# A hybrid decoder block on one core: low parts of the convolution weights by accumulating transfers, heads' products out of their banks by ScalarE

## The chip, the core and the metric

The kernel runs on one core of a Trainium2 chip. A core has five engines with a queue of instructions each: TensorE (PE) multiplies matrices into PSUM banks, VectorE (DVE), ScalarE (ACT) and GpSimd (POOL) work element by element, and SyncE (SP) mostly issues transfers. Transfers can be issued from several queues; here nearly all go out from SP, and a few from POOL. Each queue is worked off in order, and an instruction that waits for a semaphore holds up all behind it on the same engine. The metric is the time of one execution on the device in microseconds (us); the median of the runs counts.

## The reference

The block takes x of 512 positions by 1024 channels, float32, and computes

```
h   = RMSNorm(x);  P = h @ W_in
yA  = B * causal_dwconv3(C * x_in)                      short gated convolution, 512 channels
yB  = NSA(q, compressed / selected / window keys)       8 heads of 64, 2 key groups
x   = x + W_o( sigmoid(gA) * (yA @ W_A) + sigmoid(gB) * (yB @ W_B) )
x   = x + W_down( silu(causal_dwconv3(W_g RMSNorm(x)) + b) * (W_u RMSNorm(x)) )
```

W_in yields B, C, x_in, the queries, keys and values, the branch gates and the two merge gates gA and gB. Each of the convolution's twelve weight tiles (four channel tiles i, three factors j) is 1024 input rows by 128 columns, 512 KB.

## The kernel before, in words

**Two parts of each number.** All dense products are taken with float32 values that are split in two: a high part in a reduced format (fp32r), and a low part, the difference. A product is three matmuls: weight high by input high (L403), weight high by input low (L404), and, after all of these for the tile, weight low by input high (L406). So a tile of 1024 rows needs its high part for the first 16 matmuls of 512 columns and its low part only for the last eight.

**Weight tiles up to the merge.** `load_w` (L124 to 133) loads a raw tile from SP into one of three raw buffers (`wr`, L126), copies it on ACT to the high part (`wh`, two buffers in turn, L130), and subtracts raw minus high for the low part (`wl`, two buffers, L128 and L132). The subtraction runs on DVE, or on POOL with `pool=True`. For the convolution (`conv_tile`, L690) the first two tiles in order of their number, a00 and a01, use DVE and the other ten POOL; the gates (`gate_tile`, L713) and the first merge product (`mix_a_pair`, L722) use POOL always. A low buffer can be written again only when PE has ended the eight L406 matmuls of the tile two before.

**Another way, in use further on.** `dma_split` (L153 to 157) serves the last stage, the feed-forward part: ACT writes the high part (L155) and the negated raw tile into the low part's buffer (L156, with scale -1, which rounds to the reduced format); then POOL issues a transfer (L157) that reads the weights again from memory and adds them to what stands in the buffer.

**Stages.** From 0 to about 62 us three rounds of the token projection (`tok_round`, L235) fill four banks each; round 0 and round 1 hold the heads' products, 128 by 384 a bank, which leave their banks for the array `a_all` at L341 to 346 (round 0) and in `evac` (L513 to 519, round 1): banks 0 and 2 by ACT, 1 and 3 by DVE. `heads` (L534) then normalises and rotates queries and keys on DVE, takes a power -1/2 on POOL (L366), transposes on PE (L565, tiles `pqt`) and splits them into high and low parts (L570 to 576, `kL` the keys' low part). `compress` (to L504) makes the compressed keys (`kc` at L496 and L497 are its parts). From 70 to 155 us the convolution's tiles run, in the order j = 1, 2, 0 for each i, so a01, a02, a00, a11, a12, a10 and so on. The attention (`attend`, L586) is issued ahead of them in the program and its operations are laid among the matmuls of the convolution and of the gates until 312 us. Then come the second merge product (`pmb`, weights `wh_bo`, loaded by `ring_w`, L166 to 171, in buffers of a pool that opens when the attention's pool closes), the output product, and from 390 us on the feed-forward part.

**What sets the order.** The kernel is built under a context that schedules by a simulated timeline: the order of the instructions on each engine follows from that simulation and not from the text alone. Any change of an operation's engine or kind can therefore move operations of other stages on all engines.

Of the kernel before, what the change touches and what calls it, by code (L numbers as in the profile page):

```python
# [11 lines left out]
F32 = mybir.dt.float32  # L12
F32R = mybir.dt.float32r
I32 = mybir.dt.int32
AF = mybir.ActivationFunctionType
# [4 lines left out]
D = 1024  # L20
# [41 lines left out]
N_AB = 384  # L62
# [20 lines left out]
def tile_block(ctx: ExitStack, tc: tile.TileContext, xT, pos, par, par2, w_tok, w_a3, w_gate, w_ao, w_bo, w_o,  # L83
               w_ff, w_dn, c_w1, out):
    nc = tc.nc
# [25 lines left out]
    def d_bank(name):  # L111
        return bank("d", name, 2)
# [8 lines left out]
        return bank("o", name, 1)  # L121


    def load_w(src, n, name, pool=False):  # L124

        raw = pa.tile([P, TOKC], F32, name=f"wr_{name}", tag="wr", bufs=NWR)  # L126
        hi = hi_tile(name)
        lo = pa.tile([P, D], F32R, name=f"wl_{name}", tag="wl", bufs=2)  # L128
        nc.sync.dma_start(raw[:, 0:n], src)
        nc.scalar.activation(hi[:, 0:n], raw[:, 0:n], AF.Copy)  # L130
        e = nc.gpsimd if pool else nc.vector
        e.tensor_sub(lo[:, 0:n], raw[:, 0:n], hi[:, 0:n].bitcast(F32))  # L132
        return hi, lo

    def load_taps(src, name):
# [17 lines left out]
    def dma_split(h, l, raw, src, dst=None):  # L153

        nc.scalar.activation(h, raw, AF.Copy)  # L155
        nc.scalar.activation(l, raw, AF.Copy, scale=-1.0)  # L156
        nc.gpsimd.dma_start(l if dst is None else dst, src, accum_op=ALU.add)  # L157
# [32 lines left out]
    def hi_tile(name):  # L190
        n_hi.append(name)
        i = 1 - len(n_hi) % 2
        return pa.tile([P, TOKC], F32R, name=f"wh_{name}", tag=f"wh{i}", bufs=1)
# [143 lines left out]
    banks_a = tok_round(0, first_slot)  # L337
# [2 lines left out]
    nc.vector.tensor_add(sq_sum[0][:, 0], sq_sum[0][:, 0], sq_sum[0][:, 1])  # L340
    for t in range(NT):  # L341
        dst = a_all[:, t * 12 * HD + N_AB:(t + 1) * 12 * HD]
        if t % 2 == 0:
            nc.scalar.activation(dst, banks_a[t][:, 0:N_AB], AF.Copy)
        else:
            nc.vector.tensor_copy(dst, banks_a[t][:, 0:N_AB])

    ident = const([P, P], "ident")
    make_identity(nc, ident)
# [50 lines left out]
    def dense(acc, units, first=True, last=True):  # L400

        for i, (wh, wl, xh, xl) in enumerate(units):
            nc.tensor.matmul(acc, wh, xh, start=first and i == 0, stop=False)  # L403
            nc.tensor.matmul(acc, wh, xl, start=False, stop=False)  # L404
        for i, (wh, wl, xh, xl) in enumerate(units):
            nc.tensor.matmul(acc, wl, xh, start=False, stop=last and i == len(units) - 1)  # L406

    def w_units(w, xh, xl, nk, k0=0, koff=0):
        wh, wl = w
        return [(wh[:, (koff + k) * P:(koff + k + 1) * P], wl[:, (koff + k) * P:(koff + k + 1) * P],  # L410
                 xh[:, k0 + k, :], xl[:, k0 + k, :]) for k in range(nk)]
# [101 lines left out]
    def evac(banks):  # L513
        for t in range(NT):
            dst = a_all[:, t * 12 * HD:t * 12 * HD + N_AB]
            if t % 2 == 0:
                nc.scalar.activation(dst, banks[t][:, 0:N_AB], AF.Copy)
            else:
                nc.vector.tensor_copy(dst, banks[t][:, 0:N_AB])

    def values(tt, acc):
        r = r1[:, tt:tt + 1]
# [164 lines left out]
    def f_tile(name):  # L687
        return pm.tile([P, S + 2], F32, name=name, tag="f", bufs=NF_T)

    def conv_tile(i):  # L690
        accs = []
        for j in (1, 2, 0):
            w = load_w(w_a3[2 + 3 * i + j], D, f"a{i}{j}", pool=3 * i + j > 1)
            acc = d_bank(f"pa{i}{j}")
            dense(acc, w_units(w, xg_h, xg_l, KD))
            if j == 1:
                cs_ = f_tile(f"cs{i}")[:, 0:S]
                nc.vector.tensor_mul(cs_, acc, r1sq)
            elif j == 2:
                u = f_tile(f"u{i}")  # L700
                nc.gpsimd.memset(u[:, 0:2], 0.0)
                nc.vector.tensor_mul(u[:, 2:], acc, cs_)
                t = f_tile(f"ct{i}")[:, 0:S]
                causal_conv(t, u, par_sb[:, CAW + 3 * i:CAW + 3 * i + 3])
                nc.gpsimd.tensor_mul(t, t, r1b)
            else:
                nc.vector.tensor_mul(t, acc, t)
                nc.scalar.activation(ya_h[:, i, :], t, AF.Copy)
                nc.vector.tensor_sub(ya_l[:, i, :], t, ya_h[:, i, :].bitcast(F32))
# [1 line left out]


    def gate_tile(j, t):  # L713
        w = load_w(w_gate[j], D, f"g{j}", pool=True)
        acc = d_bank(f"pg{j}")
        dense(acc, w_units(w, xg_h, xg_l, KD))
        nc.vector.tensor_mul(t, acc, r1b)
        nc.scalar.activation(t, t, AF.Tanh, scale=0.5)
# [3 lines left out]
    def mix_a_pair(i):  # L722
        for j in (2 * i, 2 * i + 1):
            mix_a[j] = f_tile(f"ma{j}")[:, 0:S]
            gate_tile(j, mix_a[j])
        w = load_w(w_ao[i], D, f"ao{i}", pool=True)
        for n, j in enumerate((2 * i, 2 * i + 1)):
            acc = d_bank(f"pma{j}")
            dense(acc, w_units(w, ya_h, ya_l, 4, koff=4 * n))
            nc.vector.scalar_tensor_tensor(mix_a[j], mix_a[j], 1.0, acc, op0=ALU.add, op1=ALU.mult)  # L730
# [43 lines left out]
    for i in range(4):  # L774
# [3 lines left out]
        w = ring_w(w_bo[i], f"bo{i}")  # L778
# [33 lines left out]
    for n, j in enumerate(O_ORDER):  # L812
        w = ring_w(w_o[j], f"o{j}")
# [261 lines left out]
```

## Time and profile before

| | |
|---|---|
| time, median of three runs | 727.26 us (726.14 to 728.48) |
| the profiled execution's own time, and its span | 729.73 us, 728.0 us |
| mean granted TensorE clock | 0.994 |
| PE busy | 715.6 us (98%) |
| DVE, ACT, POOL busy | 542.7 (75%), 426.4 (59%), 196.2 us (27%) |
| POOL, low parts of the convolution (L132) | ten of 2350 to 2688 ns, 24.5 us |
| DMA, mean rate over the span | 138 GB/s |

The profile comes from one execution of its own; the span runs from its first to its last instruction. "L132" is a line of the kernel above. In a row of the waits stand the engine that waits, its tile and line, who ended the wait, the sum in us, how often, and the longest. A row of the timeline has start, length, engine, line, operation, the tiles (written <- read), and in brackets the idle time ahead with its releaser. PEld is the load of weights into TensorE, which overlaps the matmuls. A matmul's length in the timeline is its latency; the next one starts before it ends.

### The profile page before, as it was taken

How to read it: one execution, taken by the hardware profiler on the slowest of the kernel's cores; microseconds unless marked ns; L12 is line 12 of the kernel's file. 1: busy time of each engine (PE TensorE's matmuls, PEld its weight loads, DVE VectorE, ACT ScalarE, POOL GpSimd, SP SyncE). 2: the span in 40 equal slices, each digit the busy share in tenths (PEclk: the TensorE clock that was granted, in tenths of full speed). 3: DMA queues.
4: the chain of work that ended last, by engine and by line, in shares of the span. 5: the costliest groups of instructions: out<-in, count | busy, mean ns of one | idle time of the engine just before them, and what ended most of it. 6: DMA issues, size and time to landing. Idle time of an engine off the chain costs nothing.

```text
span 728.0 us, 11411 instructions
## 1 busy us (share of the span) xinstructions
PE 715.6 (98%) x4309; PEld 638.0 (88%) x4309; DVE 542.7 (75%) x977; ACT 426.4 (59%) x724; POOL 196.2 (27%) x176
## 2 busy tenths in 40 slices
PE   9999998999999999989999999999999999999997
PEld 9999877888888888868789999999999999999986
DVE  6987998776566676446696879998787877878643
ACT  8525532886577687433575777666655566656530
POOL 3232544333433344316111212211221112211110
PEclk9999999999999999989999999999999999999999
DMA  7323322111122111052666699897878768795575
GB/s 269 97 91 124 109 87 86 59 59 58 59 75 70 59 59 59 1 202 87 206 168 147 147 226 206 230 205 188 196 185 215 194 166 211 172 219 108 114 144 149
DMA packets 39703, 100.24 MB, mean 138 GB/s; under 512 B 3808, under 2 KB 9056, under 8 KB 39648
## 3 DMA queue, kind: packets, MB, share of 16 engines
q1 hardware_dynamic: 26528, 70.41, 29.1%
q0 software_dynamic: 12832, 28.84, 23.1%
q8 instruction: 34, 0.56, 0.3%
q10 hardware_dynamic: 288, 0.26, 0.1%
q14 instruction: 21, 0.17, 0.1%
HBM read 97.40 MB, written 2.10 MB: 137 GB/s over the span
## 4 chain that ended last, share of the span: by engine, by line
PE 87%; DVE 6%; ACT 2%; DMA 2%; issue 2%; POOL 2%; ACTq 0%; DVEq 0%; POOLq 0%; SPq 0%
PE p L403 8%; PE p L404 8%; PE p L406 8%; PE pdn L406 5%; PE pdn L404 5%; PE pdn L403 5%; PE pg L403 4%; PE pg L404 4%; PE pg L406 4%; PE pt L653 2%; PE pa L406 2%; PE pa L404 2%; PE po L406 2%; PE pa L403 2%; PE po L403 2%
## 5 line engine op out<-in xcount | busy, mean ns | idle before, releaser
L403 PE MATMUL p<-xf_h,sh 128*128 128x256 f32 x336 | 80.7, 277 | 0.1
L404 PE MATMUL p<-xf_l,sh 128*128 128x256 f32 x336 | 80.7, 277 | 0.0
L404 PE MATMUL pdn<-al,wh_d 128*128 128x512 f32 x176 | 68.8, 391 | 0.0
L403 PE MATMUL pdn<-ah,wh_d 128*128 128x512 f32 x176 | 68.5, 390 | 0.0
L149 ACT ACTIVATE sh<-s 128x1024 fp32r<-128x1024 f32 x44 | 46.2, 1057 | 38.1 <-PE p L404 24.5
L157 POOL DMA_DIRECT2D wl_s<-in_w_ff_dram x22 | 19.7, 895 | 167.2 <-ACT wl_s L156 155.1
L403 PEld LDWEIGHTS p<-xf_h,sh 128*128 128x128 f32 x336 | 63.0, 188 | 0.5 <-ACT sh L149 0.5
L404 PEld LDWEIGHTS p<-xf_l,sh 128*128 128x128 f32 x336 | 63.0, 188 | 0.0
L150 DVE TENSOR_TENSOR sl<-s,sh 128x1024 fp32r<-128x1024 f32 x44 | 53.5, 1217 | 8.7 <-ACT sh L149 8.7
L155 ACT ACTIVATE wh_s<-wr_s 128x1024 fp32r<-128x1024 f32 x22 | 23.3, 1058 | 54.0 <-PE pdn L404 50.1
L406 PE MATMUL p<-xf_h,sl 128*128 128x256 f32 x336 | 51.7, 277 | 0.1
L404 PE MATMUL pg<-xg_l,wh_g 128*128 128x512 f32 x128 | 50.6, 395 | 0.0
L403 PE MATMUL pg<-xg_h,wh_g 128*128 128x512 f32 x128 | 50.4, 394 | 0.0
L132 POOL TENSOR_TENSOR wl_g<-wr_g,wh_g 128x1024 fp32r<-128x1024 f32 x16 | 38.5, 2409 | 41.3 <-ACT wh_g L130 14.9
L406 PE MATMUL pdn<-ah,wl_d 128*128 128x512 f32 x176 | 47.7, 389 | 0.0
L157 POOL DMA_DIRECT2D wl_d<-in_w_dn_dram x22 | 26.6, 1211 | 77.2 <-ACT wl_d L156 67.5
L626 ACT ACTIVATE e<-sc,mx 128x512 f32<-128x512 f32 (+3 forms) x64 | 33.3, 524 | 21.4 <-DVE mx L625 16.6
L406 PEld LDWEIGHTS p<-xf_h,sl 128*128 128x128 f32 x336 | 44.6, 188 | 0.5 <-DVE sl L150 0.3
L994 DVE TENSOR_TENSOR x<-x,pdn 128x512 f32<-128x512 f32 x48 | 32.7, 681 | 16.2 <-PE pdn L406 15.5
L657 DVE TENSOR_TENSOR pl<-pt,ph 128x512 fp32r<-128x512 f32 x40 | 27.3, 684 | 19.2 <-ACT ph L656 19.1
L403 PE MATMUL p<-xf_h,wh_s 128*128 128x256 f32 x168 | 40.5, 276 | 0.0
L404 PE MATMUL p<-xf_l,wh_s 128*128 128x256 f32 x168 | 40.5, 276 | 0.0
(348 smaller groups left out, 2158.5 us busy)
## 6 DMA issues: line engine op xcount, KB each, us to landing
wr_s<-in_w_ff_dram SPq DMA_DIRECT2D x44, 512.0 KB, 5.0
wl_s<-in_w_ff_dram POOLq DMA_DIRECT2D x22, 512.0 KB, 7.7
wr_d<-in_w_dn_dram SPq DMA_DIRECT2D x22, 512.0 KB, 7.0
wl_d<-in_w_dn_dram POOLq DMA_DIRECT2D x22, 512.0 KB, 8.4
wr_g<-in_w_gate_dram SPq DMA_DIRECT2D x16, 512.0 KB, 3.4
wr_a<-in_w_a_dram SPq DMA_DIRECT2D x12, 512.0 KB, 3.5
tl<-in_w_ff_dram POOLq DMA_DIRECT2D x22, 256.0 KB, 7.2
wr_o<-in_w_o_dram SPq DMA_DIRECT2D x8, 512.0 KB, 3.5
```

The source lines that it names most:

```text
L132: e.tensor_sub(lo[:, 0:n], raw[:, 0:n], hi[:, 0:n].bitcast(F32))
L149: hi = nc.scalar.activation(h, v, AF.Copy)
L150: nc.vector.tensor_sub(l, v, h.bitcast(F32))
L155: nc.scalar.activation(h, raw, AF.Copy)
L157: nc.gpsimd.dma_start(l if dst is None else dst, src, accum_op=ALU.add)
L403: nc.tensor.matmul(acc, wh, xh, start=first and i == 0, stop=False)
L404: nc.tensor.matmul(acc, wh, xl, start=False, stop=False)
L406: nc.tensor.matmul(acc, wl, xh, start=False, stop=last and i == len(units) - 1)
L626: nc.scalar.activation(e[:, i, 0:nk], sc[:, o:o + nk], AF.Exp, bias=mx[:, i], accum_out=sums[:, i])
L653: nc.tensor.transpose(pt[:, i * P:(i + 1) * P], e[:, i, kt * P:(kt + 1) * P], ident)
L657: nc.vector.tensor_sub(pl, pt, ph.bitcast(F32))
L994: nc.vector.tensor_add(xj, xj, acc)
```

## The change

`load_w` takes the engine by name, and a third way, "dma", calls `dma_split`; ten of the twelve convolution tiles use it in place of POOL's subtraction. The low parts of the gates and of the first merge product stay on POOL, those of a00 and a01 on DVE. In the second part of the change all four banks of the heads' products leave by ACT, in both rounds. No computed value is left out: the low part is again raw minus high, now as a sum in which the negated raw value was rounded and the raw value was added.

```diff
-    def load_w(src, n, name, pool=False):
+    def load_w(src, n, name, by="vector"):
...
         nc.sync.dma_start(raw[:, 0:n], src)
-        nc.scalar.activation(hi[:, 0:n], raw[:, 0:n], AF.Copy)
-        e = nc.gpsimd if pool else nc.vector
-        e.tensor_sub(lo[:, 0:n], raw[:, 0:n], hi[:, 0:n].bitcast(F32))
+        if by == "dma":
+            dma_split(hi[:, 0:n], lo[:, 0:n], raw[:, 0:n], src)
+        else:
+            nc.scalar.activation(hi[:, 0:n], raw[:, 0:n], AF.Copy)
+            e = nc.gpsimd if by == "pool" else nc.vector
+            e.tensor_sub(lo[:, 0:n], raw[:, 0:n], hi[:, 0:n].bitcast(F32))
         return hi, lo
...
         dst = a_all[:, t * 12 * HD + N_AB:(t + 1) * 12 * HD]
-        if t % 2 == 0:
-            nc.scalar.activation(dst, banks_a[t][:, 0:N_AB], AF.Copy)
-        else:
-            nc.vector.tensor_copy(dst, banks_a[t][:, 0:N_AB])
+        nc.scalar.activation(dst, banks_a[t][:, 0:N_AB], AF.Copy)
...
             dst = a_all[:, t * 12 * HD:t * 12 * HD + N_AB]
-            if t % 2 == 0:
-                nc.scalar.activation(dst, banks[t][:, 0:N_AB], AF.Copy)
-            else:
-                nc.vector.tensor_copy(dst, banks[t][:, 0:N_AB])
+            nc.scalar.activation(dst, banks[t][:, 0:N_AB], AF.Copy)
...
-            w = load_w(w_a3[2 + 3 * i + j], D, f"a{i}{j}", pool=3 * i + j > 1)
+            w = load_w(w_a3[2 + 3 * i + j], D, f"a{i}{j}", by="dma" if 3 * i + j > 1 else "vector")
...
-        w = load_w(w_gate[j], D, f"g{j}", pool=True)
+        w = load_w(w_gate[j], D, f"g{j}", by="pool")
...
-        w = load_w(w_ao[i], D, f"ao{i}", pool=True)
+        w = load_w(w_ao[i], D, f"ao{i}", by="pool")
```

In the changed kernel `dma_split` has the lines L158 (high), L159 (negated) and L160 (transfer); lines behind L516 are three lower than before (L705 is then L702, L664 is L661).

The schedule gives a new order on every engine. First POOL in the convolution stage, before; `qst` are the powers of `heads`, `ct` the convolved tile, scaled here, `u` the two zero columns ahead of its input:

```order
L366 TENSOR_TENSOR qst13_832<-qst13_832,mhalf_296 128x6
L132 TENSOR_TENSOR wl_a02_2276<-wr_a02_2274,wh_a02_2275 128x1024
L366 TENSOR_TENSOR qst12_851<-qst12_851,mhalf_296 128x6
L701 MEMSET u0_2305 128x2
L132 TENSOR_TENSOR wl_a11_2349<-wr_a11_2347,wh_a11_2348 128x1024
L366 TENSOR_TENSOR qst11_870<-qst11_870,mhalf_296 128x6
L366 TENSOR_TENSOR qst10_889<-qst10_889,mhalf_296 128x6
L132 TENSOR_TENSOR wl_a12_2382<-wr_a12_2380,wh_a12_2381 128x1024
L705 TENSOR_TENSOR ct0_2308<-ct0_2308,rb_n1_313 128x512
```

And the same place in the changed order:

```order
L366 TENSOR_TENSOR qst13_832<-qst13_832,mhalf_296 128x6
L366 TENSOR_TENSOR qst12_851<-qst12_851,mhalf_296 128x6
L160 DMA wl_a02_2276<-in_w_a3_dram 128x1024
L698 MEMSET u0_2306 128x2
L366 TENSOR_TENSOR qst11_870<-qst11_870,mhalf_296 128x6
L160 DMA wl_a11_2350<-in_w_a3_dram 128x1024
L366 TENSOR_TENSOR qst10_889<-qst10_889,mhalf_296 128x6
L160 DMA wl_a12_2384<-in_w_a3_dram 128x1024
L702 TENSOR_TENSOR ct0_2309<-ct0_2309,rb_n1_313 128x512
```

The transfers of a02 and a11 stand behind the powers qst12 and qst11, which the subtractions stood ahead of; a12 stays behind qst10 and ahead of the scaling.

Second, ACT at the same place in the changed order. L571 and L572 copy the keys' high parts, L567 the queries', L537 squares for the next token tile:

```order
L158 ACTIVATE wh_a11_2349<-wr_a11_2348 128x1024
L567 ACTIVATE qT2_786<-pqt20_787 64x128
L537 ACTIVATE t_11_868<-a_all_93 128x384
L567 ACTIVATE qT3_815<-pqt30_816 64x128
L537 ACTIVATE t_10_887<-a_all_93 128x384
L571 ACTIVATE kHH_321<-pqt20_787 64x2x128
L572 ACTIVATE kHH_321<-pqt20_787 64x2x128
L159 ACTIVATE wl_a11_2350<-wr_a11_2348 128x1024
L571 ACTIVATE kHH_321<-pqt30_816 64x2x128
```

The negated copy of a11 is the one row that is new among these: it stands seven operations behind the high part of its tile, between the key copies of two token tiles.

Third, PE at the end of the attention, before: `po10` is the attention's last product (of group 1, query tile 0), `pg15` the last gate, `pmb0` the first of the second merge:

```order
L664 MATMUL po10_2122<-pl1000_2227,v_t_328 128x512
L404 MATMUL pg15_3441<-xg_l_91,wh_g15_3436 128x512
L403 MATMUL pg15_3441<-xg_h_90,wh_g15_3436 128x512
L404 MATMUL pg15_3441<-xg_l_91,wh_g15_3436 128x512
L406 MATMUL pg15_3441<-xg_h_90,wl_g15_3437 128x512 x8
L403 MATMUL pmb0_3156<-y0_996,wh_bo0_3152 128x512
```

And in the changed order, where seven more pairs of L403 and L404 for `pg15` are left out:

```order
L661 MATMUL po10_2122<-pl1000_2227,v_t_328 128x512
L406 MATMUL pg14_3418<-xg_h_90,wl_g14_3414 128x512
L403 MATMUL pg15_3451<-xg_h_90,wh_g15_3446 128x512
L404 MATMUL pg15_3451<-xg_l_91,wh_g15_3446 128x512
...
L406 MATMUL pg15_3451<-xg_h_90,wl_g15_3447 128x512 x8
L403 MATMUL pmb0_3166<-y0_996,wh_bo0_3162 128x512
```

Between the attention's last product and the second merge there were 3 + 8 = 11 gate matmuls; now there are 1 + 16 + 8 = 25. From `pmb0` on PE's order is the same in both.

## The prediction

> **What bounds the kernel now.** The page comes first. TensorE (PE) is busy for 98% of the span, so time can be won only where PE stands still or runs slowly. The waits of PE then name every stop:
>
> ```profile
> PE   715.6 (98%) x4309; PEld 638.0 (88%) x4309; DVE 542.7 (75%) x977; ACT 426.4 (59%) x724; POOL 196.2 (27%) x176
> ...
> PE pmb L403 <- ACT wh_bo L149: 2.6, 1, 2.6
> PE ph L499 <- DVE kc L497: 1.9, 1, 1.9
> ...
> PE pqt L565 <- DVE kL L576: 1.2, 1, 1.2
> ...
> PE pa L403 <- DVE ct L707: 0.2, 1, 0.2
> ```
>
> Third, the table by stretch puts them in place (length, then busy time of PE, PEld, DVE, ACT and POOL, the granted clock, the DMA share, GB/s):
>
> ```profile
> 80.00:100.00 20.00, 18.55 (x87) 14.92 (x86) 18.65 (x40) 10.77 (x23) 12.49 (x7) 1.00 0.32 105
> 100.00:120.00 20.00, 18.06 (x84) 14.40 (x84) 18.10 (x39) 6.20 (x13) 9.29 (x7) 1.00 0.24 80
> 120.00:140.00 20.00, 20.00 (x97) 16.68 (x96) 14.11 (x29) 11.76 (x24) 8.87 (x6) 1.00 0.16 53
> 140.00:160.00 20.00, 20.00 (x103) 16.81 (x103) 16.39 (x35) 16.15 (x33) 6.62 (x5) 1.00 0.18 58
> 160.00:300.00 140.00, 140.00 (x732) 118.64 (x731) 92.33 (x254) 97.52 (x242) 51.60 (x37) 1.00 0.18 60
> 300.00:325.00 25.00, 22.42 (x90) 18.00 (x89) 7.48 (x10) 9.58 (x17) 3.55 (x3) 0.86 0.43 147
> ```
>
> From 80 to 120 us, the convolution stage, PE idles 1.45 + 1.94 = 3.39 us, just the three waits on DVE (1.2, 0.2, 1.9). From 300 to 325 us it idles 2.58 us, and the clock drops to 0.86 of full. From 160 to 300 us it never stops: a cheaper low part is worth nothing there.
>
> **The convolution stage: why DVE is late.** The timeline of DVE and POOL around the first stop, with the spread of the same DVE line over the kernel, and DVE at the second:
>
> ```profile
> 88.88 2.32 DVE L558 TENSOR_TENSOR t<-t,qst 128x384 f32<-128x384 f32 x1
> ...
> 88.11 2.67 POOL L132 TENSOR_TENSOR wl_a<-wr_a,wh_a 128x1024 fp32r<-128x1024 f32 x1
> ...
> L558 DVE TENSOR_TENSOR t<-t,qst x8: 543/547/2319, 42.2 to 92.3; 128x384 f32<-128x384 f32 x8
> ...
> 114.25 2.42 DVE L497 TENSOR_TENSOR kc<-hb,kc 64x64 fp32r<-64x64 f32 x1
> ...
> 114.24 2.35 POOL L132 TENSOR_TENSOR wl_a<-wr_a,wh_a 128x1024 fp32r<-128x1024 f32 x1 [0.33 <-issue]
> ```
>
> An operation that takes 0.547 us in the median took 2.32 us beside a subtraction of POOL, and ended soon after it (91.20 against 90.78). The low part of a key, kL, stands behind it on DVE, and PE waits for that. At 114.25 us a subtraction of 64x64 took 2.42 us, from the start of POOL's subtraction to its end, and PE waits for its result, kc. DVE lost 1.77 us at the first place and, by the far larger operation's 0.547 us, at least 1.87 us at the second: as much as PE waited, or more, since kL's other delays came from the same queue. The change takes these subtractions off POOL, so I remove both stops: **-3.4 us** (not below -3.39, all the idle there; not above 0). In their place POOL issues transfers of 0.86 to 1.31 us. The rows of such transfers in the last stage (minimum, median and maximum in ns; then the median from issue to landing, over the kernel and for two single issues at 403.5 and 539.5 us):
>
> ```profile
> L156 ACT ACTIVATE wl_s<-wr_s x22: 1038/1041/1054, 379.4 to 672.6; 128x1024 fp32r<-128x1024 f32 x22
> ...
> L157 POOL DMA_DIRECT2D wl_s<-in_w_ff_dram x22: 856/909/912, 380.8 to 673.9; - x22
> L157 POOL DMA_DIRECT2D wl_d<-in_w_dn_dram x22: 1188/1203/1310, 422.0 to 710.2; - x22
> ...
> wl_s<-in_w_ff_dram POOLq DMA_DIRECT2D x22, 512.0 KB, 7.7
> wl_d<-in_w_dn_dram POOLq DMA_DIRECT2D x22, 512.0 KB, 8.4
> ...
> wl_s<-in_w_ff_dram POOLq DMA_DIRECT2D x1, 512.0 KB, 5.4
> ...
> wl_s<-in_w_ff_dram POOLq DMA_DIRECT2D x1, 512.0 KB, 6.4
> ```
>
> **The new chain of a low part.** Ten times 1.04 us of negated copies (10.4 us) go to ACT, ten issues of about 0.9 us to POOL in place of ten subtractions of 2.4 us. The wait moves: PE now needs the transfer to have landed. It lands 5.4 us after its issue with no other transfer near, 6.4 us with one read of 512 KB issued just ahead, and 7.7 to 8.4 us in the median of the crowded last stage. The traffic of 80 to 140 us (53 to 105 GB/s, DMA share 0.16 to 0.32) is that of a quiet place, so I take 5.4 to 6.4. Two tiles are tight:
>
> ```profile
> 80.71 0.94 PE L406 MATMUL pa<-xg_h,wl_a 128*128 128x512 f32 x3
> 90.55 1.98 PE L406 MATMUL pa<-xg_h,wl_a 128*128 128x512 f32 x8
> ...
> 79.00 1.30 PE L406 MATMUL pa<-xg_h,wl_a 128*128 128x512 f32 x5
> ...
> 84.30 1.37 POOL L366 TENSOR_TENSOR qst<-qst,mhalf 128x6 f32<-128x6 f32 x1
> ...
> 69.84 1.06 ACT L130 ACTIVATE wh_a<-wr_a 128x1024 fp32r<-128x1024 f32 x1
> 82.43 0.38 ACT L575 ACTIVATE kHH<-pqt 64x256 fp32r<-64x256 f32 x1
> ```
>
> Tile a11 takes the low buffer that a02 leaves at 81.65 us. Its negated copy stands behind the key copy that ends at 82.81 us, so it ends near 83.9; POOL issues it behind a power of 1.37 us, near 84.5. It lands from 89.9 (5.4 us) to 92.9 us (8.4 us) and PE wants it at 90.55: a stall of 0 to 2.4 us, 0.4 by a landing in 6.4 us. Tile a02: high part done 70.90, negated copy 71.94, again a power first, issue near 72.7 (the wait for DVE ahead of that power gets shorter), landing 78.1 to 81.1 against 79.00: 0 to 2.1 us, by my value 0 to 0.1. The other eight have 0.8 us or more to spare by the same reckoning. I add **+0.4 us** (0 to 4.5).
>
> Here a rule speaks against the change. The Trainium skill, "SBUF — State Buffer", section "SBUF: two separate sides", says that descriptors of a transfer issued by GpSimd can't be written while DVE runs an operation in a two-port mode. The 44 issues above all took 0.86 to 1.31 us with DVE busy for 75% of the span, so the trace doesn't show it; were an issue held up by the 0.45 us between these two, tile a11 would stall 0.85 us, and the sum would be 0.45 us worse.
>
> **Behind the negated copies on ACT** stand key copies, exponentials and probability copies. ACT is busy 10.77, 6.20 and 11.76 us of 20 in this stage. From 160 to 300 us, where PE has no gap, the attention's operations stand 3 to 9 us of matmuls earlier among the gates' than before, so what feeds them must be earlier too. No row shows a price; I bound it by 0 and by 2.1 us, two negated copies that nothing hides, and take nearer to the first **+0.4 us**, since the table has no gap there now.
>
> **The heads' products.** Four DVE copies of 0.55 us become ACT copies of 0.49 us:
>
> ```profile
> L346 DVE COPY a_all<-pj_s x1: 545/545/545, 23.0 to 23.0; 128x384 f32<-128x384 f32 x1
> ...
> L344 ACT ACTIVATE a_all<-pj_s x2: 492/492/492, 21.8 to 22.8; 128x384 f32<-128x384 f32 x2
> ```
>
> The list of PE's waits has no row for these banks, so DVE's relief is worth 0; two copies in one round now follow each other on ACT, 0.98 us later at worst, under matmuls of other banks. I take 0; the bounds are 0 and 2 us (four such copies uncovered).
>
> **The end of the attention, which the change doesn't name.** PE's timeline, the chain of waits, SP's wait for the same transfer, and the stretch at half clock:
>
> ```profile
> 312.01 0.40 PE L664 MATMUL po<-pl,v_t 128*128 128x512 f32 x1
> 312.94 1.98 PE L406 MATMUL pg<-xg_h,wl_g 128*128 128x512 f32 x8
> 317.49 0.79 PE L403 MATMUL pmb<-y,wh_bo 128*128 128x512 f32 x1 [2.58 <-ACT wh_bo L149]
> ...
> 312.50 3.81 DMA wr_bo<-in_w_bo_dram
> 316.38 1.06 ACT wh_bo L149
> ...
> SPq L168 <- PE po L664: 27.9, 1, 27.9
> ...
> 316.89:323.72 6.83, 6.23 (x15) 4.88 (x16) 3.58 (x3) 3.04 (x4) 0.00 (x0) 0.50 0.90 314
> ```
>
> The weights of the second merge product can't be loaded until the attention's last product has freed their place. From its start (312.01) to their first use (317.49) pass 5.48 us. Eight matmuls with a latency of 0.39 us took 1.98, so one follows the other by 0.227 us; the 11 gate matmuls that stand between fill 2.5 us, and PE stops for 2.58. In the changed order 25 stand there: with the product itself 26 x 0.227 = 5.90 us. The stop is covered with 0.4 us to spare: **-2.6 us** (0 if the attention ends 3 us later against the gates; the waits of the transfer are the same). The clock then was 0.50 for 6.83 us, in which 15 matmuls started; at full clock these are 3.4 us. The first of them began 0.6 us into the stretch, so their 6.2 us were 2.8 too many. Without a stop I expect no half clock: **-2.8 us** (0 to -2.8).
>
> The Trainium skill, "TensorE: Matmul & The Clock Gate", section "Part 1: The HAM clock gate", says that the gate watches a free-running window of 3.4 us. A 2.58 us stop would then cost the half clock only by its phase, in some executions and not in others; by this rule the gain at this place would be 2.6 us in some executions and 5.4 in others. This trace, with its half clock right behind a shorter stop than 3.4 us, agrees with it as far as one case can.
>
> **Sum.** -3.4 + 0.4 + 0.4 - 2.6 - 2.8 = -8.0 us. The span of 728.0 becomes 720.0, the profiled execution's own 729.73 becomes 721.7. That execution lies 2.47 us above the median of the runs (727.26; 726.14 to 728.48); the same difference on the median gives **719.3 us**.
>
> **Rivals.**
> 1. The half clock is a matter of the single execution. For it: the profiled execution is slower than all three runs by 1.2 us or more. Against: the difference may as well be the profiler's. The median then never paid the 2.8: 722.1 us.
> 2. The low parts land late, as in the last stage (8.4 us). For: ten more reads of 512 KB. Against: the low DMA share. 4.5 us of stalls instead of 0.4: 723.4 us.
> 3. The attention's end comes as late as before, because its chain through ACT and DVE, and not its place in the order, sets it. For: exponentials now queue behind more copies; the margin is 0.4 us. Against: PE has no gap from 120 to 310 us. Both terms, 5.4 us, fall away: 724.7 us.
> 4. The change doesn't free DVE: descriptor writing stretches the same operations. For: the issues last 0.9 us on the same engine. Against: they are less than half as long. Without the 3.4: 722.7 us.
> 5. The other side: ACT's queue. It runs in order, and each negated copy waits for PE to release the low buffer of two tiles earlier; the exponentials behind wait too, and PE then waits for them. Its price is up to 10.4 + 4 x 0.49 = 12.4 us if all of it falls on PE, 731.7 us. It outweighs the gains from 8.0 us on, two thirds of that, and shows as slower from 10.2. For: from 140 to 160 us 16.15 of ACT's 20 us are taken. Against: from 80 to 140 us 8 to 14 of 20 are free, and most of the copies stand where their buffer has long been released.
>
> **How the numbers follow.** Forecast 0.50; rivals 0.13, 0.12, 0.08, 0.05 and 0.12 in their order. 0.3% (2.2 us) is about what a measurement of this kernel can tell from no change: faster means under 725.1, slower over 729.4. Faster: 0.50 + 0.13 + 0.10 + 0.04 + 0.05 = 0.82, where of rivals 2 and 3 a part is worse than priced (stops of over 2 us that bring a half clock of their own). Same: 0.02 + 0.04 + 0.04 of rival 5 = 0.10. Slower: the rest of rival 5, 0.08. The range: with all costs at 0 the gain is 8.8 us, 718.5, and the lowest run lies 1.1 us below the median; with the cost of the four copies on DVE (2 us) counted as a gain in part, it begins at 716.5. Upward it takes in rivals 1, 2 and 4 whole and half of 3: 716.5 to 724.6. Rival 5 and the other half of 3 are left out, 0.16, and a little below.
>
> **What would show it.** Right: no wait of PE on kc or kL between 80 and 120 us and 20.0 busy in both stretches; L558 at 0.55 us eight times; no PE wait on wh_bo and granted clock 1.00 from 300 to 325 us; landings of the ten low parts of 5.4 to 6.5 us. Wrong: a row PE pa L406 waiting for a transfer (rival 2), ACT e or ph as a new releaser of PE (rival 5), a row on wh_bo (rival 3).

## The result, and the profile after

The changed kernel takes 720.15 us (six runs, 719.79 to 721.87), the kernel before, run beside it, 727.42 us (six runs, 723.92 to 729.48). The ratio is 0.9909, with a 95% interval of 0.9883 to 0.9935: faster by 0.65% to 1.17%. Forecast were 719.3 us in a range from 716.5 to 724.6. The profiled execution has a span of 718.1 us (own time 719.79), against 720.0 (721.7) in the sum.

The head of the page after, and its landings of the ten low parts:

```profile
span 718.1 us, 11433 instructions
...
PE   711.1 (99%) x4309; PEld 635.5 (89%) x4309; DVE 532.5 (74%) x973; ACT 437.7 (61%) x738; POOL 183.3 (26%) x176
...
wl_a<-in_w_a_dram POOLq DMA_DIRECT2D x10, 512.0 KB, 7.5
```

All waits of PE in that execution:

```profile
PE po L403 <- ACT mix_h L782: 1.3, 1, 1.3
PE wu L183 <- POOL ones L178: 1.1, 1, 1.1
PE pj_s L253 <- ACT wh_t L152: 0.7, 1, 0.7
PE ph L457 <- ACT qT L567: 0.3, 1, 0.3
```

The rows on `wh_bo`, `kc`, `kL` and `ct` are gone. The same stretches as before, with PE's busy time second and the granted clock behind POOL:

```profile
80.00:100.00 20.00, 20.00 (x91) 16.39 (x92) 17.02 (x44) 14.60 (x28) 7.40 (x7) 1.00 0.74 179
100.00:120.00 20.00, 20.00 (x97) 16.23 (x97) 12.90 (x39) 10.43 (x16) 5.02 (x8) 1.00 0.71 162
120.00:140.00 20.00, 20.00 (x93) 16.52 (x93) 14.31 (x35) 17.29 (x34) 4.63 (x7) 1.00 0.64 142
160.00:300.00 140.00, 140.00 (x735) 118.72 (x734) 93.83 (x249) 96.86 (x242) 51.86 (x38) 1.00 0.17 57
300.00:325.00 25.00, 25.00 (x112) 20.45 (x111) 15.00 (x18) 10.18 (x14) 9.93 (x6) 1.00 0.49 168
```

PE is busy throughout the convolution stage and around the second merge, at full clock. What has grown is the DMA share between 80 and 140 us: 0.64 to 0.74, from 0.16 to 0.32.

Where the 9.9 us between the two profiled spans went can be read from three places in the program. From the first convolution matmul to the last went 85.22 us before (69.84 to 155.06) and 81.48 after (69.99 to 151.47): 3.7 us, or 3.6 by the clock of the span, since the first starts 0.15 us later. The second merge starts at 317.49 before and 311.33 after: 6.2 us, so 2.6 more, the stop on `wh_bo`. The output product starts at 334.38 and 325.18: 3.0 us more, the half clock. The remaining 0.7 us lie in the feed-forward part, whose order is the same. A second profile of the kernel before (`b_again`, below) lacks them: from the start of the output product's last matmul to PE's end it takes 334.9 us, as the changed kernel does, against 335.8 in the first. So they belong to that one execution and not to the change.

### The profile page after: what moved, and what is told of

The parts are those of the page before. It is cut to its first block, busy times and chain, and to the rows that moved or that the text cites. A ratio compares the mean times of both kernels' runs of the same rounds, so it can differ in the third digit from the quotient of the medians.

```text
span 718.1 us, 11433 instructions
## 1 busy us (share of the span) xinstructions
PE 711.1 (99%) x4309; PEld 635.5 (89%) x4309; DVE 532.5 (74%) x973; ACT 437.7 (61%) x738; POOL 183.3 (26%) x176
## 4 chain that ended last, share of the span: by engine, by line
PE 96%; POOL 1%; DVE 1%; ACT 1%; DMA 1%; issue 0%; ACTq 0%
PE p L404 9%; PE p L406 9%; PE p L403 9%; PE pdn L404 6%; PE pdn L403 6%; PE pdn L406 6%; PE pg L403 4%; PE pg L404 4%; PE pg L406 4%; PE pa L403 3%; PE pa L406 3%; PE pa L404 3%; PE pt L650 2%; PE po L406 2%; PE po L403 2%; PE po L404 2%
## 5 line engine op out<-in xcount | busy, mean ns | idle before, releaser
L404 PE MATMUL p<-xf_l,sh 128*128 128x256 f32 x336 | 80.6, 277 | 0.0
L403 PE MATMUL p<-xf_h,sh 128*128 128x256 f32 x336 | 80.6, 277 | 0.0
L404 PE MATMUL pdn<-al,wh_d 128*128 128x512 f32 x176 | 68.8, 391 | 0.0
L403 PE MATMUL pdn<-ah,wh_d 128*128 128x512 f32 x176 | 68.6, 391 | 0.0
L404 PEld LDWEIGHTS p<-xf_l,sh 128*128 128x128 f32 x336 | 63.0, 188 | 0.1
L403 PEld LDWEIGHTS p<-xf_h,sh 128*128 128x128 f32 x336 | 63.0, 188 | 0.1
L160 POOL DMA_DIRECT2D wl_s<-in_w_ff_dram x22 | 19.5, 885 | 167.6 <-ACT wl_s L159 156.1
L158 ACT ACTIVATE wh_s<-wr_s 128x1024 fp32r<-128x1024 f32 x22 | 23.3, 1057 | 53.5 <-PE pdn L404 50.1
L403 PE MATMUL pg<-xg_h,wh_g 128*128 128x512 f32 x128 | 51.0, 398 | 0.0
L404 PE MATMUL pg<-xg_l,wh_g 128*128 128x512 f32 x128 | 50.7, 396 | 0.0
L160 POOL DMA_DIRECT2D wl_d<-in_w_dn_dram x22 | 26.5, 1203 | 77.6 <-ACT wl_d L159 70.4
L403 PE MATMUL p<-xf_h,wh_s 128*128 128x256 f32 x168 | 40.5, 277 | 0.0
L404 PE MATMUL p<-xf_l,wh_s 128*128 128x256 f32 x168 | 40.5, 277 | 0.0
L406 PEld LDWEIGHTS pdn<-ah,wl_d 128*128 128x128 f32 x176 | 33.0, 188 | 6.8
L404 PEld LDWEIGHTS pdn<-al,wh_d 128*128 128x128 f32 x176 | 33.1, 188 | 6.2
```

## The experiments

### One part of the change alone

`conv_only` takes back the second part of the change:

```diff
-        nc.scalar.activation(dst, banks_a[t][:, 0:N_AB], AF.Copy)
+        if t % 2 == 0:
+            nc.scalar.activation(dst, banks_a[t][:, 0:N_AB], AF.Copy)
+        else:
+            nc.vector.tensor_copy(dst, banks_a[t][:, 0:N_AB])
```

and the same in `evac`.

> The changed kernel, with the heads' products leaving their banks by ACT and DVE in turn as before: the low parts by transfers alone. The order of PE from the second projection round on is that of the changed kernel, 25 gate matmuls behind the attention's last product. Theory (the low parts bring all of the gain): 720 us, within 1 us of the changed kernel, no PE wait on kc, kL or wh_bo. Rival (DVE's relief from four copies of 0.55 us counts): 1 to 2 us slower than the changed kernel.

Measured: 720.42 us (719.77 to 721.87), ratio to before 0.9937 (0.9919 to 0.9955), span 718.2 against 718.1. `heads_only` makes the same edit in the other direction, in the kernel before:

```diff
-        if t % 2 == 0:
-            nc.scalar.activation(dst, banks_a[t][:, 0:N_AB], AF.Copy)
-        else:
-            nc.vector.tensor_copy(dst, banks_a[t][:, 0:N_AB])
+        nc.scalar.activation(dst, banks_a[t][:, 0:N_AB], AF.Copy)
```

> The kernel before, with the four copies of the heads' products that DVE made now on ACT, and the low parts on POOL as before. The order of PE from the third projection round on is that of before, with 11 gate matmuls behind the attention's last product. Theory (PE never waits for these banks): 725.8 us as before, within 0.3%, all stops still there. Rival (DVE's relief of 2.2 us brings the conv stage forward): 1 to 2 us less.

Measured: 727.48 us beside 727.14 of before, ratio 1.0006 (0.9983 to 1.0030), with the stops on `kL` (1.2), `kc` (1.9) and `wh_bo` (2.2) in place. The heads' copies are worth nothing that these runs can tell (the interval reaches from 1.2 us less to 2.2 us more); the low parts alone bring the gain.

### The convolution's stops: two tiles, then three

`two_tiles` is the kernel before, with the transfer for two tiles alone, and `three_tiles` adds a22 (number 8):

```diff
-            w = load_w(w_a3[2 + 3 * i + j], D, f"a{i}{j}", pool=3 * i + j > 1)
+            w = load_w(w_a3[2 + 3 * i + j], D, f"a{i}{j}", by="dma" if 3 * i + j in (5, 6) else "pool" if 3 * i + j > 1 else "vector")
```

> The kernel before, with only two low parts (tiles a12 and a20) by transfer: the two whose subtractions on POOL stood beside the stretched DVE operations at 88.9 and 114.3 us. The orders of PE, DVE and SP are those of before, instruction by instruction; ACT has two negated copies more. Theory (POOL's subtraction stretches DVE and DVE stops PE): both stops go, 3.4 us, while the stop on wh_bo (2.6 us) and the half clock behind it stay: about 724 us, and the two DVE operations take 0.55 and about 0.2 us. Rival (the gain came from the new order, not from POOL): 727 us, the stops still there.

> The kernel before with three low parts by transfer: a12, a20 and now a22, whose subtraction at 111.5 us still stretched a DVE operation to 1.70 us and left a wait of 0.8 us on kc in the kernel with two. The orders of PE, DVE and SP are those of before; 11 gate matmuls behind the attention's last product. Theory (all of the conv stage's gain comes from these subtractions beside DVE, the rest of the changed kernel's gain from the matmuls that cover the stop on wh_bo): no PE wait on kL or kc, the one on wh_bo still 2.2 to 2.6 us, executions in two groups by the clock, 720.6 and 722.3 us of span, 0.8 us under the kernel with two tiles; about 723.5 us, 3 us above the changed kernel. Rival (the other seven subtractions cost time too): no better than with two tiles.

The order of PE, DVE and SP is that of before in both. Two of PE's waits with two tiles (none is on `kL`; the lines of this kernel lie three behind those of before: L500 is L497):

```profile
PE pmb L406 <- ACT wh_bo L152: 2.3, 1, 2.3
...
PE ph L502 <- DVE kc L500: 0.8, 1, 0.8
```

DVE at the place of the first stop (L561 is L558 of before), then DVE and POOL at the place of the second, with two tiles. The subtraction of a22 still stands beside a small DVE operation, and of the two stops that were expected to go, that on `kc` has left 0.8 us:

```profile
89.00 0.56 DVE L561 TENSOR_TENSOR t<-t,qst 128x384 f32<-128x384 f32 x1
...
112.03 1.70 DVE L497 SCALAR_TENSOR_TENSOR hb<-hb,kss,par 64x64 f32<-64x64 f32 x1
113.99 0.22 DVE L500 TENSOR_TENSOR kc<-hb,kc 64x64 fp32r<-64x64 f32 x1
...
111.26 2.39 POOL L135 TENSOR_TENSOR wl_a<-wr_a,wh_a 128x1024 fp32r<-128x1024 f32 x1
```

And with three, where it does not, with two rows of PE's waits (none is on `kc` or `kL`):

```profile
L497 DVE SCALAR_TENSOR_TENSOR hb<-hb,kss,par x1: 277/277/277, 111.9 to 111.9; 64x64 f32<-64x64 f32 x1
...
PE pmb L406 <- ACT wh_bo L152: 2.3, 1, 2.3
...
PE pa L409 <- DMA wl_a<-in_w_a_dram: 0.3, 1, 0.3
```

Take a subtraction off POOL, and the DVE operation beside it returns to its own length (2.32 to 0.56 us ahead of `kL`, 1.70 to 0.28 here, 2.42 to 0.22 for `kc`), and PE's wait goes. The stop on `kL` is in all four profiles that have its subtraction on POOL at this place (before, b_again, heads_only, bo_early) and in none of the others. That mechanism is shown. Its size in the median is smaller than expected: 724.60 us with two tiles (ratio 0.9976, 0.9960 to 0.9993) and 724.56 with three (0.9979, 0.9962 to 0.9997), where 724 and 723.5 were expected. The third tile's 0.8 us did not show; 0.3 of it came back as a wait for a transfer.

### The kernel before, again

> The kernel before once more, for the clock of each execution. Theory (the stop of 2.6 us ahead of the second merge brings the half clock only by its phase): executions fall in two groups, mean granted clock 1.00 and about 0.994, the second some 3 us longer, so the runs spread over 3 us or more around 727.4 us. Rival (the half clock follows every such stop): every execution shows 0.994 and the spread has another source.

Twelve executions took 723.80 to 730.56 us (median 725.72), and their mean clock was not one number; there were three groups, where two were expected: six had 0.999 or 1.000 (spans 722.0 to 723.5), three 0.997 or 0.998 (724.5 to 725.7), three 0.994 or 0.995 (727.9 to 728.7). The profiled one has a span of 722.1 us, no half clock, and a stop on `wh_bo` all the same. Its waits:

```profile
PE pmb L403 <- ACT wh_bo L149: 2.4, 1, 2.4
PE po L403 <- ACT mix_h L785: 1.3, 1, 1.3
PE pqt L565 <- DVE kL L576: 1.2, 1, 1.2
```

The row on `kc`, 1.9 us in the first profile, is not there at all. DVE and POOL show why:

```profile
114.21 0.22 DVE L497 TENSOR_TENSOR kc<-hb,kc 64x64 fp32r<-64x64 f32 x1
...
114.27 3.02 POOL L132 TENSOR_TENSOR wl_a<-wr_a,wh_a 128x1024 fp32r<-128x1024 f32 x1 [0.39 <-issue]
```

In the first profile POOL started at 114.24 and DVE at 114.25, and DVE took 2.42 us. Here DVE started at 114.21 and POOL at 114.27; DVE took 0.22 us, and POOL 3.02 instead of 2.4. In heads_only and bo_early POOL was first again, by 0.01 and 0.02 us, and DVE took 2.42 and 2.40 us. So a few hundredths of a microsecond decide which of the two waits, and with it 1.9 us of PE's time. The Trainium skill, "SBUF — State Buffer", section "Who interferes with whom", says that a DVE instruction with two inputs in SBUF and a GpSimd instruction that reads SBUF exclude one another, and that the one that starts first keeps the shared port to its end. These executions agree with it. POOL's 0.6 us more is longer than DVE's 0.22 us; DVE's next operation, L709 (0.68 us), follows that one without a gap, and that POOL waited for both is inferred, not shown.

Over this and the other sessions 82 executions of the kernel before, these twelve among them, have their clock on record (the six beside the result have none listed): median 725.88 us (725.7 to 727.1 by session), spans 721.9 to 728.7. The profiled execution with 728.0 us, on which the sum was made, was among the slowest.

### The stop ahead of the second merge

`all_dma` takes the transfer for the gates and the first merge too, and `noraw` leaves out nine raw loads (below). Both change the number of gate matmuls behind the attention's last product:

```diff
-        w = load_w(w_gate[j], D, f"g{j}", by="pool")
+        w = load_w(w_gate[j], D, f"g{j}", by="dma")
...
-        w = load_w(w_ao[i], D, f"ao{i}", by="pool")
+        w = load_w(w_ao[i], D, f"ao{i}", by="dma")
```

> The changed kernel, with the low parts of the sixteen gates and of the four first merge weights by transfers too; POOL subtracts no weights any more. Same as the changed kernel through the convolution. The schedule now leaves one gate matmul between the attention's last product and the second merge. Theory (the stop is 5.48 us less the matmuls that stand between): a stop of about 5.0 us on wh_bo, perhaps with a half clock of 3 us behind it: 725 to 728 us, and nothing gained from 160 to 300 us, where PE had no gap. Rival (less work on POOL is worth time in the gates' stage): below 720 us.

Measured: 727.48 us (726.41 to 730.28), 7.3 us more than the changed kernel's 720.15 and slower than before (1.0029, 1.0013 to 1.0045). Nothing was gained from relieving POOL in the gates' stage: the last gate matmul starts at 311.58 us, against 311.10 in the changed kernel. The stop in three of the kernels, all_dma, noraw and two_tiles:

```profile
316.57 0.77 PE L403 MATMUL pmb<-y,wh_bo 128*128 128x512 f32 x1 [4.59 <-ACT wh_bo L152]
...
314.32 0.50 PE L410 MATMUL pmb<-y,wh_bo 128*128 128x512 f32 x1 [3.20 <-ACT wh_bo L159]
...
314.76 0.49 PE L406 MATMUL pmb<-y,wh_bo 128*128 128x512 f32 x1 [2.31 <-ACT wh_bo L152]
```

By the number n of matmuls between, against 5.48 - 0.227 (n + 1):

| kernel | n | reckoned, us | measured, us |
|---|---|---|---|
| all_dma | 1 | 5.0 | 4.59 |
| noraw | 7 | 3.7 | 3.20 |
| before, b_again, heads_only, two_tiles, three_tiles | 11 | 2.8 | 2.58, 2.40, 2.23, 2.31, 2.33 |
| changed (two profiles), conv_only, mix_dve | 25 | -0.4 | 0 in all four |

The stop follows the order. The passage from the attention's last product to the second merge hardly depends on n: it took 5.48 us in the first profile and 5.13 to 5.30 in the other six with a stop; with 25 matmuls it is 5.90, their own length. The measured stops lie a few tenths below the reckoning because of this shorter passage, and because the last matmul's latency (0.39 us, 0.16 more than the spacing) counts as busy. With eleven matmuls there is a stop in all five profiles; with 25 in none.

The half clock is another matter. The clock's records in these traces hold windows of 3.413 us (310.613 us of full clock is 91 of them, the half clocks of 3.413 and 6.827 us one and two). Where they lie against the span differs from execution to execution. Laid over the stops:

| execution | stop, from to us | most idle time in one window, us | half clock behind it, us |
|---|---|---|---|
| all_dma | 311.98 to 316.57 | 3.41 | 3.41 |
| three_tiles | 312.04 to 314.36 | 2.33 | 3.41 |
| two_tiles | 312.45 to 314.76 | 2.31 | 3.41 |
| heads_only | 315.02 to 317.25 | 2.23 | 3.41 |
| before | 314.91 to 317.49 | 1.98 | 6.83 |
| noraw | 311.11 to 314.32 | 1.69 | none |
| b_again | 312.93 to 315.33 | 1.29 | none |

A stop of 3.20 us that fell across two windows cost no half clock; one of 2.23 us inside one window did. From the start of the second merge to that of the output product pass 13.85 to 13.98 us in the six profiles without a half clock there, 15.54 to 15.61 in the four with one window and 16.89 with two: one window costs some 1.6 us. With two tiles the executions fall into two groups with nothing between: five at a clock of 0.999 or 1.000 with spans of 721.3 to 721.6 us, seven at 0.997 or 0.998 with 722.9 to 723.6. The Trainium skill, "TensorE: Matmul & The Clock Gate", section "Part 1: The HAM clock gate", states such a free-running window of 3.413 us, and the traces agree. It also puts the return to half rate behind one idle window, by which a stop of 2.58 us could never bring it; the prediction drew on the window and left this out. Here 1.98 us of idle time in one window were enough and 1.69 were not, and the measurement decides. It decides for this place only: in `bo_early`, described next, a window with 1.48 us of idle time (286.31 to 289.72 us, among short matmuls of the attention) was followed by half clock. What besides the idle time counts is open.

### Taking the wait itself away

`bo_early` (from the kernel before) and `bo_early_changed` (from the changed one) load the first tile of the second merge into buffers that don't wait for the attention:

```diff
-        w = ring_w(w_bo[i], f"bo{i}")
+        w = load_w(w_bo[i], D, f"bo{i}") if i == 0 else ring_w(w_bo[i], f"bo{i}")
```

> The kernel before, with the first weight tile of the second merge loaded into the raw and split buffers of the earlier stages, so that it doesn't wait for the attention's last product. The order is that of before through the convolution and up to the tenth gate; then the schedule lays five gates among the matmuls of the second merge. Theory (that wait costs 2.6 us and, by its phase, up to 3 us of half clock): no PE wait on wh_bo, granted clock 1.00 in every execution, the stop on kL still there and the one on kc in some executions: about 722 us against 725.8 of before, in groups some 2 us apart. The 1.3 us on mix_h may be covered too. Rival (another wait takes its place, such as the attention's last output y): 724 us or more.

> The changed kernel with the same early load for the second merge. Theory (the changed order has already covered that stop): within 1 us of the changed kernel's 720.2 us, or 1.3 us less where the gates' matmuls cover the wait on mix_h. Rival (the changed order leaves a cost at this place that the profile doesn't name): 2 us less or more.

Both theories fell; for `bo_early` the rival, another wait in its place, came true. `bo_early` took 732.56 us (ratio 1.0094, 1.0066 to 1.0122), `bo_early_changed` 728.38 (1.0029, 1.0012 to 1.0046), 8 us over the changed kernel. The wait on `wh_bo` is gone, and others stand in its place. The first and the third to fifth row of PE's waits in bo_early_changed, and its stretch from 280 to 300 us:

```profile
PE po L656 <- ACT ph L653: 1.9, 2, 1.5
...
PE pmb L403 <- ACT y L670: 1.0, 1, 1.0
PE pt L650 <- ACT e L627: 0.9, 2, 0.6
PE pmb L403 <- DVE t_all L780: 0.4, 1, 0.4
...
280.00:300.00 20.00, 15.34 (x58) 10.41 (x56) 10.73 (x35) 12.79 (x34) 3.36 (x6) 0.83 0.28 103
```

With the weights at hand early, the schedule moved gates out of the attention's end and behind the start of the second merge. The attention's last chain through ACT and DVE then had no matmuls left to run under, PE stopped 4.7 us in twenty, and the clock fell to 0.83 there. So no run takes the stop on `wh_bo` away and leaves the rest as it is: what the covered stop is worth rests on the two tables above.

### How long a low part takes to land

`noraw` lets the ten tiles share one raw tile and so leaves out nine raw loads; nine tiles then have mixed weights:

```diff
-        raw = pa.tile([P, TOKC], F32, name=f"wr_{name}", tag="wr", bufs=NWR)
+        if by == "dma" and n_raw:
+            raw = n_raw[0]
+        else:
+            raw = pa.tile([P, TOKC], F32, name=f"wr_{name}", tag="wr", bufs=NWR)
+            nc.sync.dma_start(raw[:, 0:n], src)
+            if by == "dma":
+                n_raw.append(raw)
...
-        nc.sync.dma_start(raw[:, 0:n], src)
```

> The changed kernel without nine raw loads: the ten low parts by transfer all take the raw tile of a02 for their high and negated parts (so the products of the other nine tiles are of mixed weights), while each accumulating transfer still reads its own 512 KB. Left out: the nine reads of 512 KB that SP starts when the negated copy gives a raw buffer free, just as POOL issues the accumulating transfer. Theory (that read slows the landing): the ten land in 5.4 to 6 us as the quiet ones do, against 7.5 us in the median of the changed kernel. Rival (the landing is slow for another reason, such as POOL's descriptors held up by DVE): still 7 us or more. The schedule leaves seven gate matmuls behind the attention's last product: a stop of 5.48 - 8 x 0.227 = 3.7 us on wh_bo.

The ten landings took 5.63, 5.81, 5.43, 5.52, 5.54, 5.88, 5.44, 5.42, 5.57 and 7.46 us; the last has the load of a first merge tile beside it (issued at 136.82 us, the low part at 137.09). In the changed kernel they took 5.64, 6.23, 7.99, 7.36, 7.96, 7.39, 7.58, 7.33, 8.27 and 7.92. This kernel was executed once (724.92 us, with the 3.20 us stop above). The medians in noraw's page and, behind it, the changed kernel's SP queue at one tile, with ACT's negated copy ahead:

```profile
wl_a<-in_w_a_dram POOLq DMA_DIRECT2D x10, 512.0 KB, 5.6
```

```profile
87.62 1.05 ACT L159 ACTIVATE wl_a<-wr_a 128x1024 fp32r<-128x1024 f32 x1
...
88.69 5.69 SPq L129 DMA_DIRECT2D wr_a<-in_w_a_dram  x2
...
SPq L129 <- ACT wl_a L159: 52.4, 10, 9.8
...
88.96 0.90 POOL L160 DMA_DIRECT2D wl_a<-in_w_a_dram  x1 [1.72 <-ACT wl_a L159]
```

The negated copy (87.62 to 88.67) is the last reader of the raw buffer: SP issues the next raw load at 88.69, and POOL the accumulating transfer at 88.96. Ten times SP waited for just this copy. So the two travel together, and by the medians of these two profiles that costs the low part about 2 us.

### A wait that is left

`mix_dve` moves the last two additions of the merge:

```diff
-            nc.gpsimd.tensor_add(m, m, mix_a[j])
+            (nc.vector if j > 5 else nc.gpsimd).tensor_add(m, m, mix_a[j])
```

> The changed kernel, with the last two of the eight additions that join the merge products (on POOL, 1.3 to 2.2 us each, stretched where DVE subtracts beside them) on DVE. The orders of PE, ACT and SP stay instruction by instruction. Theory (the wait of 1.3 us on mix_h ahead of the output product ends with the last of these additions): that wait is gone and the kernel 1.3 us faster than the changed one, near 719 us. Rival (DVE's own queue, with a subtraction of 1.22 us among them, takes the place of POOL): no difference.

> The changed kernel once more, beside the two others. Theory: 720.2 us, all executions within 2 us of each other and at a clock of 1.00, since no stop is left that could bring the half clock; what spread there is comes from low parts that land within 0.2 us of their first use. Rival: some executions with a lower clock or over 723 us.

Measured side by side: 720.53 us (719.38 to 721.98) with the edit and 720.75 without (six executions each). A seventh execution without it took 2537.91 us at a clock of 1.00; the record has no cause for it, and it is left out of that median and of what follows. Two of PE's waits with it:

```profile
PE p L406 <- DVE sl L153: 0.8, 1, 0.8
...
PE po L403 <- ACT mix_h L782: 0.2, 1, 0.2
```

The wait on `mix_h` fell from 1.3 to 0.2 us, but in this execution PE waits 0.8 us at 416 us, in the feed-forward part, which the changed kernel's profile does not show. Whether that belongs to the edit stays open; the times do not tell the kernels apart.

The changed kernel itself held 1.00 or 0.999 in its twelve other executions, with spans of 718.1 to 720.7 us; the repeat alone spread over 2.3 us, where 2 had been expected. The repeat shows where its spread may come from, a row that the first profile lacks:

```profile
PE pa L406 <- DMA wl_a<-in_w_a_dram: 0.5, 2, 0.3
```

## Why the prediction was right

**The direction, the range and the two causes held.** The stops on `kL` and `kc` came from POOL's subtractions beside DVE, and the stop on `wh_bo` and the half clock from the eleven matmuls behind the attention's last product. The first profile after shows each as named: no wait on either, PE busy 20.00 of 20, clock 1.00, and the DVE operation L497 at 0.22 us.

**The terms of the sum, on the profiled executions.** Convolution: -3.4 forecast, -3.6 found. Stop on `wh_bo`: -2.6 forecast, -2.6 found. Half clock: -2.8 forecast, -3.0 found. Costs: +0.8 forecast; the first profile has no wait for a transfer among PE's, the second has 0.5 us of them, and its convolution took 82.46 us against 81.48, so up to 1.0. The span of the first came out 1.9 us under the sum: 0.8 by costs that were not paid, 0.7 by the feed-forward part of the one execution before, the rest by the two sizes.

**The step that failed is the last one: "the same difference on the median".** The sum was made on an execution that had both stops in full and the longest half clock. By the mean clock of its 82 executions, 24 of before paid no half clock (0.999 or more; spans 721.9 to 724.1), 42 one window (0.996 to 0.998; 723.5 to 727.8) and 16 two (0.994 or 0.995; 725.5 to 728.7); the sorting is an estimate, from a window of 3.413 us at half clock, which lowers the mean by 0.0023. The `kc` stop was absent from one of the four profiles with that piece of the order (before, b_again, heads_only, bo_early). On the medians of all executions the gain is 725.88 - 720.30 = 5.6 us (12 executions of the changed kernel), not 8.0; beside each other in one session they gave 7.3 (727.42 and 720.15). Between the changed kernel's first profile and that of b_again lie 4.0 us of span, not 9.9. That the forecast still came within 1 us is in part luck: the median of three runs that it started from, 727.26, was itself 1.4 us above that of the 82. Rival 1 had named this: it was right that the half clock belongs to single executions, and wrong that the median never pays it, since 58 of 82 did.

**How the median's gain divides** can be bounded with the kernel of three tiles: it has lost the convolution's stops and kept the other. In one session the kernel before had a median of 725.98 us, three tiles 724.56 and the changed kernel 720.75. So some 1.4 us of the median's gain come from the convolution and some 3.8 from the rest, the covered stop and its half clock above all, where the sum had 3.4 (less 0.8) and 5.4. The division is rough: the executions behind these medians spread by 2 to 7 us, and the seven subtractions that stay on POOL with three tiles were not tried apart.

**The landing was mis-sized.** 5.4 to 6.4 us were assumed, from the low traffic before the change; 7.5 was the median. The traffic of before was the wrong row, since the change itself adds to it, and each transfer is issued with a raw load. The late landings cost little, because the need came late enough, sometimes by a hair: a02 landed at 79.83 us and was used at 79.87, a12 at 96.96 and 97.05, both without a wait in PE's list. For a02 the transfer sets the moment all the same: in the second profile it landed at 80.41 and was used at 80.45. Of the tight chains, that of a11 was worked out well (issue at 84.50 for 84.5; landing at 90.73 for 90.9; use at 90.89 with no stall). That of a02 was not: POOL's two powers ahead of it took 4.56 us, twice 1.37 would have been 2.7, and it was issued at 74.18 instead of 72.7. In the second profile it was issued at 72.94, but took 7.47 us to land.

```profile
69.67 4.56 POOL L366 TENSOR_TENSOR qst<-qst,mhalf 128x6 f32<-128x6 f32 x2 [13.05 <-DVE qst L540]
74.18 1.06 POOL L160 DMA_DIRECT2D wl_a<-in_w_a_dram  x1
...
79.87 2.11 PE L406 MATMUL pa<-xg_h,wl_a 128*128 128x512 f32 x8
90.89 2.00 PE L406 MATMUL pa<-xg_h,wl_a 128*128 128x512 f32 x8
```

Rival 2 came half true: as late as in the last stage, yes, but without its stalls of 4.5 us.

**The other rivals.** PE's timeline after, and the spreads of two lines:

```profile
305.42 0.39 PE L661 MATMUL po<-pl,v_t 128*128 128x512 f32 x1
311.33 0.39 PE L403 MATMUL pmb<-y,wh_bo 128*128 128x512 f32 x1
...
L555 DVE TENSOR_TENSOR t<-t,qst x8: 542/548/559, 42.8 to 88.5; 128x384 f32<-128x384 f32 x8
...
L160 POOL DMA_DIRECT2D wl_a<-in_w_a_dram x10: 837/875/1372, 74.2 to 135.4; - x10
```

Rival 3 (the attention's end late all the same) did not come: from its last product to the second merge pass 5.91 us, for the 5.90 forecast. Rival 4 fell: L558 (now L555) took 0.542 to 0.559 us eight times beside POOL's issues. Rival 5 fell: ACT was busy for 17.29 of 20 us from 120 to 140, and no wait of PE names an exponential. Nor did the rule show that spoke against the change (the Trainium skill, "SBUF — State Buffer", "SBUF: two separate sides"): nine of the ten issues took 0.84 to 1.06 us, and noraw's nine quiet landings of 5.4 to 5.9 us include the 5.4 of the last stage. The tenth issue, that of a11, took 1.37 us, in the second profile and in conv_only too, and 0.92 in noraw; what held it is open, and PE did not wait for it.

## What to carry to other kernels

Where an off-path engine's long operation shares a port with short ones on a path, look at the short one's spread (0.547 us in the median, 2.32 at most): an outlier marks a place to look at, and where a wait of the path stands behind it, taking away two or three of the long operations removed it. Not every outlier does: with two tiles the same line still took 1.58 us once, and PE did not wait. Before a sum is carried from a profile to a median, see whether the profiled execution is a typical one; behind the stops of 2 to 3 us on TensorE here the half clock was a matter of chance, and it went with the stop. In a kernel whose order a scheduler sets, check what any edit does to the matmuls that cover a late chain: here one edit moved 14 of them to the right place unasked, and a well-meant one moved them away for 8 us.

## What the runs showed of the hardware, unexpected

An accumulating transfer kept the DMA engines busy twice as long as a plain one of the same size. A quiet raw load from 84.2 to 87.7 us of before, and the first low part of the changed kernel from 74.1 to 79.9, by queue (packets, MB, share of 16 engines over the stretch):

```profile
q1 hardware_dynamic: 144, 0.52, 44.6%
```

```profile
q0 software_dynamic: 144, 0.52, 52.3%
```

That is 0.446 x 3.5 = 1.6 us of all sixteen engines for the plain 512 KB, and 0.523 x 5.8 = 3.0 us for the accumulating one. The stage from 80 to 140 us shows the same, before, in the changed kernel and in noraw (rate in GB/s last, DMA share ahead of it). The changed kernel has twice the rate of before and three times the share; noraw, where the accumulating transfers took the place of all but a few plain ones, has about the rate of before and twice the share:

```profile
80.00:140.00 60.00, 56.61 (x266) 46.00 (x265) 50.85 (x107) 28.73 (x59) 30.64 (x20) 1.00 0.24 79
```

```profile
80.00:140.00 60.00, 60.00 (x279) 49.13 (x280) 44.24 (x115) 42.31 (x77) 17.05 (x21) 1.00 0.70 161
```

```profile
80.00:140.00 60.00, 60.00 (x287) 49.35 (x286) 44.74 (x115) 42.80 (x79) 17.82 (x21) 1.00 0.48 89
```

All accumulating transfers here go out from POOL's queue and all plain ones from SP's, so whether the adding or the queue makes them longer was not told apart.

The second surprise is the clock: its records hold windows of 3.413 us that lie by chance. Of the seven stops ahead of the second merge, the five that put 1.98 us or more of idle time into one window cost a half clock of one or two windows, and the two with 1.69 us or less cost none. That is no threshold for other places: in bo_early 1.48 us in one window were followed by half clock.
